# Down product of a SwiGLU block: loads of the rows' tiles issued by ScalarE, and four loading steps tied to named products

## The chip, the cores and the metric

The kernel runs on one core of a Trainium2 chip. The metric is the device time of one execution in microseconds (us). Three runs of the kernel before gave 2198.46, 2200.58 and 2203.82 us; the median is 2200.58 us. A further execution, the one that was profiled, took 2203.5 us.

## The reference

A decoder trunk of two layers works on 1024 positions of width 1024 in float32. Layer 0 mixes with a short gated convolution, layer 1 with dilated attention; each is followed by a feed-forward block (FFN). The FFN's inner width is 2816, which is 22 tiles of 128.

```
def swiglu(h, w_gate, w_up, w_down):
    return (jax.nn.silu(h @ w_gate) * (h @ w_up)) @ w_down

for i in range(DEPTH):                       # DEPTH = 2
    h = rms_norm(x, mix_norm[i])
    ...                                      # x = x + mixer(h)
    h = rms_norm(x, ffn_norm[i])
    x = x + swiglu(h, ffn_w_gate[i], ffn_w_up[i], ffn_w_down[i])
return rms_norm(x, final_norm)
```

## The kernel before

**Numbers and products.** Each float32 operand is split into a high part (ScalarE, an ACTIVATE copy) and a low part (VectorE, a subtraction), and a product is three matmuls of the split parts (lines L515 to L517; L607, L609 and L610 for the smaller "deep" products). On top of that the kernel multiplies by Strassen's scheme in Winograd's form: a block product is made of seven smaller products, numbered 1 to 7 and made in the order `WINOGRAD = 1, 2, 6, 5, 7, 3, 4`.

**Gate and up.** The class `Strassen` with its subclass `Swiglu` makes gate and up in 22 units, u = 0 to 21. Each unit has products (u, m); for part of them the scheme is applied once more, and such a deep product is written m = 11 to 17 (`DEEPER` = 10 plus its number). The list `order` sets the order of all products. The last eleven are those of unit 21: (21,6), (21,5), (21,7), (21,11), (21,12), (21,15), (21,16), (21,3), (21,17), (21,13), (21,14). After (21,7) ScalarE copies the bank to memory (`save`, L521), VectorE adds the other half (L593), multiplies with the gate (L1135), and GpSimd's queue stores the 256 KB half page to DRAM (L674, "plain<-c"). Deep products are taken out of their banks by VectorE (L525).

**Down.** `down` (L728 to L755) multiplies the result by w_down, with the rows in chunks of three pairs. For each m of `WINOGRAD` it makes two products on TensorE, each taken out of its bank by an addition to x on VectorE (L736, "the x-add"). The first two products with m = 6 go to the banks that those with m = 1 used, so they wait for the x-adds of m = 1. Its weights pass through the same engines: L138 makes the high and L139 the low part of a weight tile, L186 forms the combinations.

**The rows' tiles.** The inputs of `down` come back from DRAM. The generator `feed` (L705 to L724) does this in eight steps. The step for an m takes three half pages named "hin" (128x512 float32, 256 KB) and issues their loads (L712), and then it converts the tiles of the step before: three copies on ScalarE (L507) and three subtractions on VectorE (L508). A trio below means these three instructions on one of the engines. There are 63 loads in each FFN, 126 in all.

**What sets the order.** Each engine executes its instructions in the order in which the kernel writes them, and semaphores make it wait for others. The next step of `feed` is called in two ways: `down` calls it after each pair of products, and for the first chunk `filled` calls it after certain products of unit 21 (L780). Before the change these are the five from (21,16) on: (21,16), (21,3), (21,17), (21,13), (21,14). The loads of weights (`load_raw`, L152, "raw") and of x (`load_x`, L702) are on SyncE's queue (SP), as the "hin" loads are. All half pages are taken in turn from one ring of buffers, so a load may have to wait for the last user of its buffer, which can be a store.

Of the kernel before, what the change touches and what calls it, by code (L numbers as in the profile page):

```python
# [28 lines left out]
MAXDIST = 2048  # L29
WINOGRAD = (1, 2, 6, 5, 7, 3, 4)  # L30
DEEP, DEEPER = (2, 4), 10
WARM = 10


# [61 lines left out]
def trunk(ctx: ExitStack, tc: tile.TileContext, x, gains_in, cwi, ck, cwo, wqkv, wo, relb,  # L96
          wg, wu, wd, oneh, ident, out):
    nc = tc.nc
# [11 lines left out]
    def half_page(name, dt=F32):  # L110
        return scope["pool"].tile([128, 512], dt, name=name, tag="half", bufs=scope["halves"])

    def bank():
        return psum.tile([128, 512], F32, name="bank", tag="bank")
# [44 lines left out]
    def ensure(upto):  # L159
        while op_state[0] < min(upto + 1, len(ops)):  # L160
            key = ops[op_state[0] + 1][0] if op_state[0] + 1 < len(ops) else None
            if key in sums_of:
                sums_of.pop(key)()
            made[op_state[0]] = ops[op_state[0]][1]()
            op_state[0] += 1
# [195 lines left out]
    def run(*gens):  # L361
        for _ in zip(*gens):
            pass
        for g in gens:
            for _ in g:
                pass
# [116 lines left out]
    class Strassen:  # L483
# [220 lines left out]
        def feed(self, c):  # L704

            tiles = None
            for m in WINOGRAD + (None,):
                new = None
                if m:
                    new = [half_page("hin") for k in range(self.chunk)]  # L710
                    for k in range(self.chunk):
                        nc.sync.dma_start(new[k], self.parts[c + k, m])  # L712
                if tiles:
                    lows = [self.hi(last, k, t, nc.vector)
                            for k, t in enumerate(tiles)]
                    for lo in lows:
                        lo()
                tiles, last = new, m
                if m:
                    self.b[m] = [None] * self.chunk  # L720
                    yield
# [8 lines left out]
        def down(self, c, n, feed):  # L730

            p, r = {}, {}
            later = {2: (1,), 6: (3,), 5: (4,), 7: (6,), 3: (5,), 4: (7,)}

            def add(n, h, b):
                nc.vector.tensor_tensor(out=X[n][:, half(h)], in0=X[n][:, half(h)], in1=b, op=ALU.add)  # L736

            for m in WINOGRAD:
                for k in (n, n + 2):
                    if m == 1:  # L740
                        p[k] = bank()
                    if m == 5:
                        r[k] = bank()
                    b = bank() if m == 2 else r[k] if m in (3, 5) else p[k]
                    self.mm((c, k), m, b, m in (1, 2, 5), 4)
                    add(k + (m in (5, 7, 4)), int(m in (6, 5, 7, 3)), b)
                next(feed, None)
                if c == n == 0:
                    self.load_x(*later.get(m, ()))
                    self.rest(m)  # L750
# [10 lines left out]
        def run(self, start, hooks={}):  # L761

            self.base = op_state[1]
            last = self.nu - 1

            def filled(n):
                start(n)
                if self.key != CONV:
                    self.now = n + 1
                    i = self.order.index((3, 4))  # L770
                    if n == i - 15:
                        prep.append(self.deepen(2))
                    if n == i - 5:
                        prep.append(self.deepen(4))
                    for p in prep:
                        next(p, None)
                if self.key == CONV:
                    self.below(n, last)
                else:
                    if self.order[n][0] == last and n >= self.at(last, DEEPER + 6) - self.base:  # L780
                        next(feed, None)
                    if self.order[n] == (last, DEEPER + 7):
                        self.load_x(0, 2)
                        ensure(self.at(last, DEEPER + 4) + 4)
                self.idle(n)

            prep = []
            if self.key == CONV:
                self.products(filled, hooks)
                self.first_tiles()  # L790
                return
            feed = self.feed(0)
            self.products(filled, hooks)
            for c in range(0, self.pairs, self.chunk):
                self.down(c, 0, feed)
                feed = self.feed(c + self.chunk) if c + self.chunk < self.pairs else self.feed_last()
                self.down(c, 4, feed)
            run(feed)
# [863 lines left out]
    warm = bank()  # L1662
    for _ in range(WARM):
        nc.tensor.matmul(warm[:, :128], ones, ones, start=True, stop=True)
# [158 lines left out]
```

## Time and profile before

| | |
|---|---|
| median of three runs | 2200.58 us |
| profiled execution | 2203.5 us |
| its span | 2201.7 us |
| granted clock of TensorE, mean | 0.987 |
| TensorE busy | 2143.2 us, 97% |
| VectorE busy | 1762.2 us, 80% |
| ScalarE busy | 997.6 us, 45% |
| "hin" loads | 126 of 256 KB, all on SP |

The profile lists engines as PE (TensorE), DVE (VectorE), ACT (ScalarE), POOL (GpSimd) and SP (SyncE); a "q" behind the name means its DMA queue. Times count from the start of the span. In rows of a timeline the first number is the start and the second the duration, "x3" says that three instructions stand in the row, and the bracket at the end gives the idle time of the engine before it and what ended that. The change lies at two places: from 754 us on, where the first FFN passes from gate and up to down, and from 1946 us on, where the second one does.

### The profile page before, as it was taken

How to read it: one execution, taken by the hardware profiler on the slowest of the kernel's cores; microseconds unless marked ns; L12 is line 12 of the kernel's file. 1: busy time of each engine (PE TensorE's matmuls, PEld its weight loads, DVE VectorE, ACT ScalarE, POOL GpSimd, SP SyncE). 2: the span in 40 equal slices, each digit the busy share in tenths (PEclk: the TensorE clock that was granted, in tenths of full speed). 3: DMA queues.
4: the chain of work that ended last, by engine and by line, in shares of the span. 5: the costliest groups of instructions: out<-in, count | busy, mean ns of one | idle time of the engine just before them, and what ended most of it. 6: DMA issues, size and time to landing. Idle time of an engine off the chain costs nothing.

```text
span 2201.7 us, 30568 instructions
## 1 busy us (share of the span) xinstructions
PE 2143.2 (97%) x11158; PEld 1832.0 (83%) x11158; DVE 1762.2 (80%) x3242; ACT 997.6 (45%) x1800; POOL 153.2 (7%) x202
## 2 busy tenths in 40 slices
PE   9999999899999999999999999998899999999998
PEld 7788877688888878878999998887778888878887
DVE  7898759888888798865677777868988888889886
ACT  7433426444444444435455455534544444454435
POOL 1000000010101000010111111110010101000000
PEclk9999999999999999999999999999899999999999
DMA  7222631223333374323333333443123333265432
GB/s 222 82 91 68 224 121 39 91 96 106 110 97 119 123 280 147 113 67 130 91 91 92 94 98 89 153 148 132 53 79 105 104 105 112 96 233 198 158 91 77
DMA packets 132560, 260.03 MB, mean 118 GB/s; under 512 B 47530, under 2 KB 58810, under 8 KB 132410
## 3 DMA queue, kind: packets, MB, share of 16 engines
q1 hardware_dynamic: 76410, 186.38, 26.6%
q0 software_dynamic: 14832, 48.60, 6.4%
q10 hardware_dynamic: 41168, 23.10, 3.7%
q8 instruction: 88, 1.44, 0.3%
q14 instruction: 62, 0.51, 0.1%
HBM read 188.62 MB, written 66.26 MB: 116 GB/s over the span
## 4 chain that ended last, share of the span: by engine, by line
PE 80%; DVE 11%; ACT 4%; DMA 3%; issue 2%; ACTq 0%; SPq 0%; DVEq 0%
PE bank L517 16%; PE bank L515 16%; PE bank L516 16%; PE bank L356 5%; PE bank L358 5%; PE bank L357 5%; PE bank L1446 4%; PE bank L609 2%; PE bank L610 2%; PE bank L607 2%; DVE w L139 1%; DVE b L508 1%; PE bank L1374 1%; PE bank L1373 1%; DVE x L448 1%
## 5 line engine op out<-in xcount | busy, mean ns | idle before, releaser
L515 PE MATMUL bank<-b,w 128*128 128x512 f32 x1784 | 703.9, 395 | 14.3 <-ACT b L507 6.0
L517 PE MATMUL bank<-b,w 128*128 128x512 f32 x1784 | 702.1, 394 | 15.6 <-DVE w L139 15.6
L516 PE MATMUL bank<-b,w 128*128 128x512 f32 x1784 | 701.5, 393 | 2.6 <-DVE b L508 2.1
L517 PEld LDWEIGHTS bank<-b,w 128*128 128x128 f32 x1784 | 338.9, 190 | 91.0 <-DVE w L139 20.3
L515 PEld LDWEIGHTS bank<-b,w 128*128 128x128 f32 x1784 | 339.2, 190 | 88.5 <-ACT w L138 7.5
L516 PEld LDWEIGHTS bank<-b,w 128*128 128x128 f32 x1784 | 339.0, 190 | 73.8 <-DVE b L508 2.9
L138 ACT ACTIVATE w<-combo 128x512 fp32r<-128x512 f32 (+2 forms) x464 | 235.1, 535 | 289.2 <-DVE combo L186 280.2
L139 DVE TENSOR_TENSOR w<-combo,w 128x512 fp32r<-128x512 f32 (+2 forms) x464 | 261.3, 576 | 74.6 <-ACT w L138 71.9
L521 ACT ACTIVATE part<-bank 128x512 f32<-128x512 f32 x168 | 99.5, 595 | 271.9 <-PE bank L517 268.0
L139 DVE TENSOR_TENSOR w<-raw,w 128x512 fp32r<-128x512 f32 (+2 forms) x316 | 169.2, 561 | 21.1 <-ACT w L138 19.4
L525 DVE TENSOR_TENSOR part<-part,bank 128x256 f32<-128x256 f32 (+1 forms) x348 | 159.3, 488 | 28.9 <-PE bank L517 17.1
L138 ACT ACTIVATE w<-raw 128x512 fp32r<-128x512 f32 (+2 forms) x316 | 150.1, 520 | 45.5 <-PE bank L517 11.4
L736 DVE TENSOR_TENSOR x<-x,bank 128x512 f32<-128x512 f32 x168 | 114.6, 682 | 31.2 <-PE bank L517 31.2
L356 PE MATMUL bank<-w_hi,w 128*128 128x512 f32 (+1 forms) x320 | 121.5, 380 | 0.0
L358 PE MATMUL bank<-w_hi,w 128*128 128x512 f32 (+1 forms) x320 | 119.5, 373 | 0.7 <-DVE w L139 0.7
L357 PE MATMUL bank<-w_lo,w 128*128 128x512 f32 (+1 forms) x320 | 119.6, 374 | 0.0
L448 DVE TENSOR_TENSOR x<-x,bank 128x512 f32<-128x512 f32 (+1 forms) x104 | 66.0, 642 | 62.0 <-PE bank L358 53.0
L356 PE MATMUL bank<-h_hi,w_hi 128*128 128x512 f32 x256 | 104.6, 408 | 0.6 <-ACT w_hi L138 0.6
L186 DVE TENSOR_TENSOR combo<-raw 128x512 f32<-128x512 f32 (+1 forms) x160 | 103.2, 645 | 0.0
L358 PE MATMUL bank<-h_hi,w_lo 128*128 128x512 f32 x256 | 100.1, 391 | 0.8 <-DVE w_lo L139 0.8
L357 PE MATMUL bank<-h_lo,w_hi 128*128 128x512 f32 x256 | 99.9, 390 | 0.0
L1132 ACT ACTIVATE part<-part 128x512 f32<-128x512 f32 x66 | 39.7, 628 | 111.5 <-DVE part L525 111.5
(243 smaller groups left out, 3841.3 us busy)
## 6 DMA issues: line engine op xcount, KB each, us to landing
hin<-part SPq DMA_DIRECT2D x126, 256.0 KB
raw<-in_ffn_w_gate SPq DMA_DIRECT2D x44, 512.0 KB
raw<-in_ffn_w_up SPq DMA_DIRECT2D x44, 512.0 KB
part<-sum POOLq DMA_DIRECT2D x72, 256.0 KB, 3.0
raw<-in_ffn_w_down SPq DMA_DIRECT2D x48, 384.0 KB
raw<-in_conv_w_in SPq DMA_DIRECT2D x24, 512.0 KB
x<-spill SPq DMA_DIRECT2D x24, 512.0 KB
raw<-in_attn_w_qkv SPq DMA_DIRECT2D x24, 512.0 KB
```

The lines of the kernel that those rows point to most:

```text
L138: nc.scalar.activation(hi, src, AF.Copy)
L139: eng.tensor_tensor(out=lo, in0=src, in1=hi, op=ALU.subtract)
L186: eng.tensor_tensor(out=c, in0=a, in1=b, op=op)
L356: nc.tensor.matmul(b, whi[:, a], ahi[:, s], start=first, stop=False)
L357: nc.tensor.matmul(b, whi[:, a], alo[:, s], start=False, stop=False)
L358: nc.tensor.matmul(b, wlo[:, a], ahi[:, s], start=False, stop=last)
L515: nc.tensor.matmul(b, hi[:, a], bhi, start=start and k == 0, stop=False, skip_group_check=True)
L516: nc.tensor.matmul(b, hi[:, a], blo, start=False, stop=False, skip_group_check=True)
L517: nc.tensor.matmul(b, lo[:, a], bhi, start=False, stop=k == n - 1, skip_group_check=True)
L521: nc.scalar.activation(t, b, AF.Copy)
L525: nc.vector.tensor_tensor(out=t, in0=t, in1=b, op=ALU.add)
L736: nc.vector.tensor_tensor(out=X[n][:, half(h)], in0=X[n][:, half(h)], in1=b, op=ALU.add)
```

## The change

```
+FEEDING = 5, 7, 3, DEEPER + 4
...
         def feed(self, c):
...
                     for k in range(self.chunk):
-                        nc.sync.dma_start(new[k], self.parts[c + k, m])
+                        nc.scalar.dma_start(new[k], self.parts[c + k, m])
...
                 else:
-                    if self.order[n][0] == last and n >= self.at(last, DEEPER + 6) - self.base:
+                    if self.order[n] in [(last, m) for m in FEEDING]:
                         next(feed, None)
```

All 126 "hin" loads move from SP's queue to ScalarE's, where they stand in order among its ACTIVATEs. In each FFN four steps instead of five are made in unit 21: after (21,5), (21,7), (21,3) and (21,14). The first loads m = 1. The second loads m = 2 and converts m = 1, the third loads m = 6 and converts m = 2, the fourth loads m = 5 and converts m = 6. Before, the trios of m = 1, 2, 6 and 5 were called after (21,3), (21,17), (21,13) and (21,14). The trios of m = 5, 7, 3 and 4 now fall into `down`, behind the products of m = 1, 2, 6 and 5; before, those of 7, 3 and 4 did, behind 1, 2 and 6. The order on TensorE and GpSimd is unchanged. Lines of the kernel after are one higher.

The first place is ScalarE behind the product (21,7), in the first FFN. `part<-bank` saves this product, `w<-combo` are high parts of weights, `b<-hin` is a trio, and `part_0_2` to `part_2_2` are the tiles for m = 2 of pairs 0, 1 and 2. Semaphores called DMASW count GpSimd's transfers, DMAHW those of SP and ScalarE. Before:

```order
L521 ACTIVATE part<-bank 128x512 [waits DMASW1_49,PE_49]
L138 ACTIVATE w<-combo 128x256 x2
L138 ACTIVATE w<-combo 128x512 [waits DVE_49,Activation_49]
L138 ACTIVATE w<-combo 128x256 x4
L507 ACTIVATE b<-hin 128x512 [waits DMAHW5_49,Activation_49]
L507 ACTIVATE b<-hin 128x512 [waits DMAHW6_49]
L507 ACTIVATE b<-hin 128x512 [waits DMAHW7_49]
```

After:

```order
L522 ACTIVATE part<-bank 128x512 [waits DMASW6_49,PE_49,Activation_49]
L713 DMA hin<-part_0_2_182 128x512 [waits DVE_49]
L713 DMA hin<-part_1_2_189 128x512 [waits DMASW0_49,DVE_49]
L713 DMA hin<-part_2_2_196 128x512 [waits DMASW3_49]
L508 ACTIVATE b<-hin 128x512 [waits DMAHW3_49]
L508 ACTIVATE b<-hin 128x512 [waits DMAHW4_49]
L508 ACTIVATE b<-hin 128x512 [waits DMAHW5_49]
L139 ACTIVATE w<-combo 128x256 x2
L139 ACTIVATE w<-combo 128x512 [waits DVE_49]
L139 ACTIVATE w<-combo 128x256 x4
```

Three loads and the trio of m = 1 now stand ahead of the weights of the deep product (21,16), the row `w<-combo 128x256 x2`. The count of DMASW3 that the third load waits for is that of GpSimd's store of the product (21,7), "plain<-c": the load's buffer is the one that this store reads.

The second place is VectorE at the same product. `c` is the result of (21,7), the row `combo<-raw,combo` and the one behind it make the weights of (21,16), and the first `part<-part,bank` empties the bank of (21,11), which (21,16) then uses. Before:

```order
L593 TENSOR_TENSOR c_6767<-part,bank 128x512
L1135 TENSOR_TENSOR c_6654<-c_6767,c_6654 128x512
L186 TENSOR_TENSOR combo<-raw,combo 128x512
L139 TENSOR_TENSOR w<-combo,w 128x256 x2
L525 TENSOR_TENSOR part<-part,bank 128x256 x2
```

After:

```order
L594 TENSOR_TENSOR c_6773<-part,bank 128x512
L1136 TENSOR_TENSOR c_6654<-c_6773,c_6654 128x512
L509 TENSOR_TENSOR b<-hin,b 128x512 x3
L187 TENSOR_TENSOR combo<-raw,combo 128x512
L140 TENSOR_TENSOR w<-combo,w 128x256 x2
L526 TENSOR_TENSOR part<-part,bank 128x256 x2
```

The trio of m = 1 has come in ahead of the weights and the emptying of the bank.

The third place is VectorE from the emptying of the banks of (21,13) and (21,14) to the first x-adds of `down`. Before:

```order
L525 TENSOR_TENSOR part<-part,bank 128x256 x2
L508 TENSOR_TENSOR b<-hin,b 128x512 x3
L525 TENSOR_TENSOR part<-part,bank 128x256 x2
L1135 TENSOR_TENSOR part<-part 128x512 x2
L508 TENSOR_TENSOR b<-hin,b 128x512 x3
L186 TENSOR_TENSOR combo<-raw 128x384
L186 TENSOR_TENSOR combo<-combo,raw 128x384
L139 TENSOR_TENSOR w<-combo,w 128x384
L736 TENSOR_TENSOR x<-x,bank 128x512
```

After:

```order
L526 TENSOR_TENSOR part<-part,bank 128x256 x4
L1136 TENSOR_TENSOR part<-part 128x512 x2
L509 TENSOR_TENSOR b<-hin,b 128x512 x3
L187 TENSOR_TENSOR combo<-raw 128x384
L187 TENSOR_TENSOR combo<-combo,raw 128x384
L140 TENSOR_TENSOR w<-combo,w 128x384
L737 TENSOR_TENSOR x<-x,bank 128x512
```

One trio is left here where two stood; the one of m = 5 has gone behind the first x-adds. Further up, between (21,3) and (21,13), the trios of m = 1 and m = 2 stood before, and only that of m = 2 stands there now.

More of the change, by code (lines that the diff above doesn't have):

```diff
@@ L31 @@
 DEEP, DEEPER = (2, 4), 10
+FEEDING = 5, 7, 3, DEEPER + 4
 WARM = 10
@@ L711, in feed @@
                     for k in range(self.chunk):
-                        nc.sync.dma_start(new[k], self.parts[c + k, m])
+                        nc.scalar.dma_start(new[k], self.parts[c + k, m])
                 if tiles:
@@ L779, in filled @@
                 else:
-                    if self.order[n][0] == last and n >= self.at(last, DEEPER + 6) - self.base:
+                    if self.order[n] in [(last, m) for m in FEEDING]:
                         next(feed, None)
```

## The prediction

> **What bounds the kernel now.** I read the page first, then TensorE's waits around the two places of the change, then the timelines of TensorE and VectorE there. The page's first lines:
>
> ```profile
> span 2201.7 us, 30568 instructions
> PE 2143.2 (97%) x11158; PEld 1832.0 (83%) x11158; DVE 1762.2 (80%) x3242; ACT 997.6 (45%) x1800; POOL 153.2 (7%) x202
> ```
>
> TensorE works 97% of the span, so only its idle time, and the time in which it runs at half clock, can be won or added. What it waited for in the first FFN's transition and the start of its down product (740 to 960 us), then in the second's (1900 to 2140 us); columns are total, count, longest:
>
> ```profile
> PE bank L515 <- ACT b L507: 3.0, 1, 3.0
> PE bank L607 <- DVE part L525: 2.0, 1, 2.0
> ```
>
> ```profile
> PE bank L515 <- ACT b L507: 3.0, 1, 3.0
> PE bank L607 <- ACT b L507: 2.0, 1, 2.0
> ```
>
> Each transition has two gaps, and both FFNs show the same. No row names a load: TensorE never waits here for weights or rows' tiles to arrive, so bringing loads forward has no wait of its own to remove. TensorE's timeline places the gaps:
>
> ```profile
> 774.60 0.36 PE L607 MATMUL bank<-t,w 128*128 128x256 f32 x1 [2.01 <-DVE part L525]
> ...
> 787.47 0.52 PE L515 MATMUL bank<-b,w 128*128 128x512 f32 x1 [3.02 <-ACT b L507]
> 787.79 0.63 PE L516 MATMUL bank<-b,w 128*128 128x512 f32 x1
> ...
> 791.19 0.39 PE L515 MATMUL bank<-b,w 128*128 128x512 f32 x1
> 791.42 0.40 PE L516 MATMUL bank<-b,w 128*128 128x512 f32 x1
> ```
>
> The second gap has a tail. From 787.47 to 791.19 stand nine matmuls in 3.72 us; at the step of 0.23 (791.19 to 791.42) they would take 2.07. So 1.65 us more are lost. The clock over that stretch, and after a longer gap elsewhere; the columns behind the window are its length, busy times of PE, PEld, DVE, ACT and POOL, PE's granted clock, DMA share and GB/s:
>
> ```profile
> 787.80:791.20 3.40, 3.40 (x10) 2.63 (x9) 3.40 (x7) 3.02 (x7) 0.00 (x0) 0.50 1.03 415
> ...
> 1511.50:1518.00 6.50, 4.54 (x15) 3.96 (x16) 3.79 (x6) 2.58 (x5) 0.00 (x0) 0.50 0.21 81
> ```
>
> VectorE's timeline says what the gaps wait for:
>
> ```profile
> 761.89 0.69 DVE L593 TENSOR_TENSOR c<-part,bank 128x512 f32<-128x512 f32 x1 [2.27 <-ACT part L521]
> 762.61 0.69 DVE L1135 TENSOR_TENSOR c<-c,c 128x512 f32<-128x512 f32 x1
> 763.22 0.68 DVE L186 TENSOR_TENSOR combo<-raw,combo 128x512 f32<-128x512 f32 x1
> ...
> 764.49 0.75 DVE L525 TENSOR_TENSOR part<-part,bank 128x256 f32<-128x256 f32 x2
> ...
> 769.76 0.69 DVE L525 TENSOR_TENSOR part<-part,bank 128x512 f32<-128x512 f32 x1 [0.59 <-PE bank L517]
> ...
> 771.09 1.89 DVE L508 TENSOR_TENSOR b<-hin,b 128x512 fp32r<-128x512 f32 x3
> ...
> 774.04 0.75 DVE L525 TENSOR_TENSOR part<-part,bank 128x256 f32<-128x256 f32 x2
> ...
> 783.31 1.89 DVE L508 TENSOR_TENSOR b<-hin,b 128x512 fp32r<-128x512 f32 x3
> ...
> 786.64 0.68 DVE L736 TENSOR_TENSOR x<-x,bank 128x512 f32<-128x512 f32 x1
> ```
>
> From 769.76 to the x-add VectorE is not idle. The first gap ends when the bank of (21,17) is emptied (774.04), behind the trio of m = 1 (771.09). The second ends at 787.47, right behind the x-add of 786.64 to 787.32, which frees the bank that the first product of m = 6 takes; the profile names ScalarE's L507, but no trio made then belongs to that product. This x-add stands behind the trios of m = 1, 2, 6 and 5.
>
> **The change part by part: what it wins.** Between the end of (21,3) and the first x-add VectorE loses two trios, those of m = 1 and m = 5, 2 x 1.89 = 3.78 us. The second gap, 3.02, is smaller, so it closes, and with it goes its tail. The gain is 3.0 + 1.65 = 4.7 us in each FFN. The first gap stays: the trio of m = 2 stands where that of m = 1 stood. What is late next there is TensorE itself: VectorE then has 3.78 - 3.02 = 0.8 us to spare.
>
> **What it adds: a wait on ScalarE.** The second step is called right behind (21,7). On ScalarE its three loads and the trio of m = 1 stand ahead of the weights of (21,16), and the third load waits for GpSimd's store of (21,7). Before, the same wait stood on SP, where nothing but loads is queued behind it. The store on POOL, its landing time in the first and in the second FFN, that of an earlier store with little traffic, and SP's wait for it before:
>
> ```profile
> 763.60 0.54 POOL L674 DMA_DIRECT2D plain<-c  x1 [19.99 <-DVE c L1135]
> ```
>
> ```profile
> plain<-c POOLq DMA_DIRECT2D x1, 256.0 KB, 3.9
> ```
>
> ```profile
> plain<-c POOLq DMA_DIRECT2D x1, 256.0 KB, 3.6
> ```
>
> ```profile
> plain<-c POOLq DMA_DIRECT2D x1, 256.0 KB, 2.5
> ```
>
> ```profile
> SPq L712 <- DMA plain<-c: 0.9, 1, 0.9
> ```
>
> The store lands at L = 763.60 + 2.5 to 3.9 = 766.1 to 767.5. I take 3.4, nearer to the rows of this very store, hence L = 767.0; it is a bit under 3.6 because part of the loads now runs ahead of it. Does a DMA issue on ScalarE's queue hold back the ACTIVATE behind it? Rows of ScalarE elsewhere, and the line of its other stores (minimum, median, maximum in ns):
>
> ```profile
> 1003.99 7.32 ACTq L1591 DMA_DIRECT2D spill<-x  x5
> 1011.36 2.96 ACT L138 ACTIVATE w_hi<-raw 128x1024 fp32r<-128x1024 f32 x3 [6.96 <-DMA spill<-x]
> ```
>
> ```profile
> L1203 ACTq DMA_DIRECT2D spill<-x x32: 326/326/343, 305.5 to 1539.0; - x32
> ```
>
> It does: ScalarE was idle for 6.96 us while five issues went out, and its next ACTIVATE started 0.05 us behind the last. So from about 763.7 to L ScalarE stands. VectorE stands as well, since the trio of m = 1 is its next row and needs ScalarE's copies, and then TensorE, whose (21,16) needs weights and a bank from both. ScalarE's rows:
>
> ```profile
> 761.75 0.71 ACT L138 ACTIVATE w<-combo 128x256 fp32r<-128x256 f32 x2
> ...
> 765.77 1.66 ACT L507 ACTIVATE b<-hin 128x512 fp32r<-128x512 f32 x3
> ```
>
> and (21,16) on TensorE:
>
> ```profile
> 765.37 0.28 PE L607 MATMUL bank<-t,w 128*128 128x256 f32 x1
> ```
>
> The chain behind L: issue of the load 0.33, ScalarE's trio 1.66, the third subtraction on VectorE 1.89 / 3 = 0.63, together 2.6. Then as before: from L186 at 763.22 to the bank's emptying at 764.49 1.27 us, and from there to (21,16) at 765.37 0.88 us. (21,16) starts at L + 4.75 = 771.75 instead of 765.37: a new gap of 6.4 us, with L's bounds 5.5 to 6.9. ScalarE's weights for it (0.71) fit beside VectorE's work. The gap passes on in full, since at 769.76 VectorE waited for TensorE.
>
> **The clock behind the new gap.** It is longer than both gaps above. Behind that of 3.02 the clock was 0.50 for 3.4 us, costing 1.65; behind the row at 1511.50 it was 0.50 for 6.5 us, costing 3.2 in a dense stretch. I take 1.7, with 0 and 3.2 as bounds: VectorE empties the banks of (21,3) and (21,17) here and may be late anyway. In the Trainium skill, the page "TensorE: Matmul & The Clock Gate" (section "Part 1: The HAM clock gate") says that an idle window of about 3.4 us brings the half clock and a busy one of the same length ends it. By that rule the cost is 1.7; by the longer row it is 3.2, and 3.0 more in the sum over two FFNs. The row at 787.47 differs from the page in another point: 3.02 us of idling sufficed.
>
> **The later steps.** In `down` the trio of m = 5 comes on top of VectorE's work, 1.89 us. Windows of the first FFN, same columns:
>
> ```profile
> 790.00:820.00 30.00, 30.00 (x131) 24.75 (x130) 27.05 (x51) 11.16 (x23) 0.00 (x0) 0.98 0.59 195
> 820.00:850.00 30.00, 30.00 (x134) 24.84 (x133) 29.93 (x55) 15.74 (x32) 0.00 (x0) 1.00 0.52 173
> ```
>
> Up to 820 VectorE has 2.95 us left and TensorE misses nothing, so most of it is hidden; if that cover is gone it costs all 1.89. I take 0.5 of 0 to 1.9. ScalarE gets three issues of 0.33, 1.0 us, in each step of `down`. In 820 to 850 it was idle for 14.26 us; a step has two products of nine matmuls, 4.1 us, so that is 1.9 us a step. I take nothing; the other end is the last rival.
>
> **The sum.** For each FFN 6.4 + 1.65 + 0.5 - 4.7 = +3.9 us; bounds 5.5 + 0 + 0 - 4.7 = +0.8 and 6.9 + 3.2 + 1.9 - 4.7 = +7.3. Two FFNs: +7.8, from +1.6 to +14.6. The profiled execution took 2203.5 us, its span 2201.7; it would become 2211.3. It lies 2.9 above the median of the runs, so the median becomes 2200.58 + 7.8 = 2208.4, from 2202.2 to 2215.2. About 0.3%, or 6.6 us, is the least that a measurement of this kernel can tell from no change.
>
> **The rivals.** *The wait does not hold ScalarE (not slower).* If ACTIVATEs pass the waiting issue, or the store lands before ScalarE gets there, no gap opens at (21,16), and only the gain is left: 2 x (0.5 - 4.7) = -8.4, 2192.2 us. For it speaks that L1203's issues cost 0.33 us each; against it the idle 6.96 us above. It decides from a gap of about 2.5 us (with its half clock) downward, for then the gain is larger. In the Trainium skill, "DMA: Bandwidth & Descriptors" (section "Issuing engines are not separate DMA queues") says that issuing from several engines saves only the time of issuing, as all share the same DMA engines. Read as the whole price of moving the loads, the sum by it is that of this rival; the 6.96 us show that the page leaves out what stands behind the issue.
>
> *Gain and loss cancel.* The gap is at its short end (5.5) and the clock does not drop, or VectorE's own lateness swallows the drop: +0.8 in each FFN, 2202.2 us. For it speaks the store of 2.5 us; against it both rows of this store.
>
> *ScalarE is late all through `down`.* In the first rows above ScalarE's five issues took 7.32 us, 1.46 each, not 0.33. If the loads' issues are slowed like that, or wait for buffers, the copies come late for VectorE, which is full from 820 on. At 0.4 us in each of 34 steps (42 groups of three loads, less the eight in unit 21) this adds 14 us: 2222 us. Against it speak three issues of 256 KB in a step, not eight, and ScalarE's idle half. It decides from the point at which a step's issues exceed the 1.9 us that ScalarE has left in it.
>
> **How the numbers follow.** Forecast 0.60, of which I put 0.37 above +6.6 us and 0.23 below it; no hold 0.15; cancelled 0.17; ScalarE late 0.08. Slower by over 0.3%: 0.37 + 0.08 = 0.45. Within 0.3%: 0.23 + 0.17 = 0.40. Faster: 0.15. The range takes in the bounds of the sum and reaches half into the first rival, and some way toward the last: 2192 to 2218.
>
> **What would show it.** In the profile of the changed kernel: ScalarE and VectorE idle from about 764 to 767 us with the store's landing as releaser; a gap of 5.5 to 6.9 us at (21,16) and half clock behind it; the gap of 2.0 still ahead of (21,14); none of 3.0 ahead of the first m = 6; the same in the second FFN. The prediction is wrong if (21,16) starts without a gap, if the 3.0 us remain, or if new gaps run through `down`.

## The result, and the profile after

The kernel after took 2213.41 us (median of 6 runs, 2209.69 to 2214.59), the kernel before 2200.32 us in the same comparison. The ratio is 1.0056, 95% interval 1.0043 to 1.0069: the change makes the kernel slower by about 13 us, where 7.8 were forecast. The profiled execution took 2211.88 us.

What TensorE waits for in the kernel after, first in the first FFN (740 to 960 us), then in the second (1900 to 2140 us); the columns are total, count, longest:

```profile
PE bank L608 <- DVE part L526: 8.0, 2, 6.0
PE bank L516 <- DVE x L737: 0.9, 1, 0.9
```

```profile
PE bank L608 <- DVE part L526: 8.1, 2, 6.1
PE bank L516 <- DVE x L737: 0.9, 1, 0.9
```

The wait of 3.0 ahead of the first product with m = 6 is gone. The gap of 2.0 ahead of (21,14) is still there, and a gap of 6.0 stands beside it. TensorE's timeline shows where:

```profile
766.78 0.55 PE L608 MATMUL bank<-t,w 128*128 128x256 f32 x1 [6.01 <-DVE part L526]
...
778.31 0.36 PE L608 MATMUL bank<-t,w 128*128 128x256 f32 x1 [2.01 <-DVE part L526]
```

The first is (21,16), the second (21,14). ScalarE's timeline shows the cause of the first:

```profile
756.55 0.60 ACT L522 ACTIVATE part<-bank 128x512 f32<-128x512 f32 x1 [2.29 <-issue]
756.57 5.86 ACTq L713 DMA_DIRECT2D hin<-part  x3
762.48 1.67 ACT L508 ACTIVATE b<-hin 128x512 fp32r<-128x512 f32 x3 [5.33 <-DMA plain<-c]
```

Three issues stretch over 5.86 us, and ScalarE does nothing for 5.33 us until GpSimd's store lands, as the bracket says. VectorE stands with it, for its next rows need these copies; then come the weights and the bank for (21,16):

```profile
763.14 1.90 DVE L509 TENSOR_TENSOR b<-hin,b 128x512 fp32r<-128x512 f32 x3 [4.54 <-ACT b L508]
764.95 0.69 DVE L187 TENSOR_TENSOR combo<-raw,combo 128x512 f32<-128x512 f32 x1
765.55 0.76 DVE L140 TENSOR_TENSOR w<-combo,w 128x256 fp32r<-128x256 f32 x2
766.22 0.75 DVE L526 TENSOR_TENSOR part<-part,bank 128x256 f32<-128x256 f32 x2
```

The granted clock (the number ahead of the DMA share and GB/s at the end) behind the gap of 6.0 and behind that of 2.0:

```profile
766.80:770.20 3.40, 3.40 (x14) 3.30 (x15) 3.40 (x11) 3.40 (x10) 0.00 (x0) 0.50 0.98 380
...
778.30:781.70 3.40, 3.39 (x15) 3.21 (x16) 3.37 (x9) 0.37 (x1) 0.00 (x0) 0.54 0.02 5
```

The gap of 2.0 is now followed by a stretch at half clock. In the kernel before the same gap was not:

```profile
774.60:778.17 3.57, 3.57 (x21) 3.20 (x22) 3.54 (x8) 0.00 (x0) 0.00 (x0) 1.00 1.02 405
```

The order on TensorE is unchanged, so each matmul of the kernel before has its counterpart after. The difference of their start times, taken from the end of (21,15) on, shows step by step where the time goes. The kernel before had come to this place 4.76 us later in its profiled execution, a difference that arose in the first 330 us, far ahead of the change; the steps do not contain it.

| matmul | first FFN, start before and after | step | step in the second FFN |
|---|---|---|---|
| (21,16), first | 765.37, 766.78 | +6.17 | +6.28 |
| (21,17), first | 769.56, 773.27 | +2.30 | +2.38 |
| (21,14), first | 774.60, 778.31 | 0.00 | 0.00 |
| down, the 10th | 778.17, 783.43 | +1.54 | +1.56 |
| down, first of m = 6 | 787.47, 789.56 | -3.17 | -3.18 |
| nine further | 791.19, 791.60 | -1.68 | -1.61 |
| later in down | 811.86, 813.47 | +1.21 | +1.30 |
| sum | | +6.4 | +6.7 |

Both FFNs together give +13.1, which is also the difference of the medians.

### The profile page after: what moved, and what is told of

Same layout as the page of the kernel before. It is cut to its first block, busy times and chain, and to the rows that moved or that the text cites. A ratio compares the mean times of both kernels' runs of the same rounds, so it can differ in the third digit from the quotient of the medians.

```text
span 2209.8 us, 30489 instructions
## 1 busy us (share of the span) xinstructions
PE 2146.1 (97%) x11158; PEld 1835.3 (83%) x11158; DVE 1763.3 (80%) x3242; ACT 1001.2 (45%) x1800; POOL 153.6 (7%) x202
## 4 chain that ended last, share of the span: by engine, by line
PE 50%; issue 30%; DVE 10%; ACT 4%; POOL 3%; DMA 2%; ACTq 0%; SPq 0%; POOLq 0%; DVEq 0%
PE bank L518 8%; PE bank L516 8%; PE bank L517 8%; PE bank L359 5%; PE bank L357 5%; PE bank L358 5%; PE bank L1447 4%; POOL part L698 2%; DVE b L509 2%; DVE w L140 1%; PE bank L1375 1%; PE bank L1374 1%; POOL part L679 1%; DVE x L449 1%; PE bank L1315 1%
```

## The experiments

Each kernel was timed against the kernel before in five rounds; the ratio is that of the kernel to before. An edit can shift line numbers by one or two, so the x-add is L736 to L739.

**The steps alone.** The kernel after, with the loads on SP.

```
-                        nc.scalar.dma_start(new[k], self.parts[c + k, m])
+                        nc.sync.dma_start(new[k], self.parts[c + k, m])
```

> The four named steps of the kernel after, but the loads of the rows' tiles on SP's queue as in the kernel before. Theory (the cost comes from ScalarE standing behind one load that waits for a store): with the wait back on SP only the trio of m = 1 (1.9 us on VectorE) stands ahead of (21,16), so the gap there falls from 6.0 to about 1.9 us with little or no half clock behind it, the gap of 3.0 ahead of m = 6 and its tail stay away (-4.5), the later gap in the down product costs 0.5 to 1.1: for each FFN -1.5 to -2, a median of 2196 to 2198 us, slightly faster than before. Rival (the places of the steps cost, whatever the queue): still slower than before by 8 us or more, over 2208.

Measured: 2196.66 us, ratio 0.9986 (0.9976 to 0.9995). TensorE's waits in the first FFN:

```profile
PE bank L608 <- DVE part L526: 3.4, 2, 2.0
```

The two waits are 2.0 ahead of (21,14) and the rest, 1.4, at (21,16). The steps at their new places win 3 to 4 us; the queue turns that into a loss.

**The queue alone.** The kernel before, with the loads on ScalarE.

```
-                        nc.sync.dma_start(new[k], self.parts[c + k, m])
+                        nc.scalar.dma_start(new[k], self.parts[c + k, m])
```

> The steps of the kernel before, with all 126 loads on ScalarE's queue. Theory: the load that needs the buffer of GpSimd's store comes two products later, when the store has landed, so ScalarE is not held: both gaps of before (2.0 and 3.0 us) stay and nothing of 6 us appears at (21,16); the median stays within 3 us of before, 2198 to 2204. Rival (the issues on ScalarE make its copies late all through the down product): new gaps in down, over 2208 us.

Measured: 2200.46 us, ratio 1.0000 (0.9992 to 1.0009). The 126 issues on ScalarE cost nothing where none of them waits long. So neither half of the change costs anything by itself.

**One load back on SP.** The kernel after, but the load that waits for the store on SP.

```
-                        nc.scalar.dma_start(new[k], self.parts[c + k, m])
+                        (nc.sync if (c, k, m) == (0, 2, 2) else nc.scalar).dma_start(new[k], self.parts[c + k, m])
```

> The kernel after, with one load of 63 in each FFN put back on SP's queue: the third of m = 2 for pairs 0 to 2, which waits for the store. Theory: this one load holds ScalarE, so the gap at (21,16) falls from 6.0 to about 2 us and most of the half clock behind it goes; with -4.5 for the gap and tail ahead of m = 6 and +1.1 in down this is -1.5 to +0.5 for each FFN, a median of 2197 to 2202 us. Rival (the other 62 loads and the trio, not this wait): little changes, over 2208 us.

Measured: 2206.10 us, ratio 1.0023 (1.0014 to 1.0032), between the two expectations. The gap at (21,16) fell to 3.6 and 3.3 us, not to 2. ScalarE's and VectorE's timelines say why:

```profile
758.87 1.68 ACT L508 ACTIVATE b<-hin 128x512 fp32r<-128x512 f32 x3 [1.85 <-DVE c L1136]
```

```profile
759.54 1.89 DVE L509 TENSOR_TENSOR b<-hin,b 128x512 fp32r<-128x512 f32 x3 [1.07 <-ACT b L508]
762.45 0.69 DVE L187 TENSOR_TENSOR combo<-raw,combo 128x512 f32<-128x512 f32 x1 [1.01 <-DMA plain<-c]
```

The second load, still on ScalarE, waits for VectorE's product with the gate. And the store's buffer was given to another tile: VectorE itself now waits for the store, 1.01 us. The edit did not take the wait away but moved it; it could not settle the question. The profiled execution took 2202.28 us, the shortest of the eleven, so these gaps and the clock behind them need not stand for the median.

**The third step later.** The kernel after, with its third step behind (21,17).

```
-FEEDING = 5, 7, 3, DEEPER + 4
+FEEDING = 5, 7, DEEPER + 7, DEEPER + 4
```

> The kernel after, with its third step called after (21,17) instead of (21,3). VectorE then empties the bank of (21,17) ahead of the trio of m = 2, so the gap of 2.0 us ahead of (21,14) should close. Theory on the clock (the second stretch at half clock is set off by that gap): 2.0 + 1.5 us go in each FFN, a median of about 2206.5 us. Rival (the half clock there is a late effect of the gap of 6 us): the 2.0 us go but 1.5 stay, about 2209.5 us.

Measured: 2212.86 us, ratio 1.0055 (1.0043 to 1.0068): nothing won on the kernel after, so both forecasts of the time failed. TensorE's waits in the first FFN:

```profile
PE bank L608 <- DVE part L526: 7.1, 2, 6.9
PE bank L516 <- DVE x L737: 4.0, 4, 1.6
```

The gap ahead of (21,14) did close (7.1 less 6.9 is 0.2), but waits for x-adds grew from 0.9 to 4.0 us in down, and the gap at (21,16) was longer by 0.9. On the clock the trace sides with the theory all the same: behind (21,14), where the kernel after showed 0.54, the granted clock was full, and so it was in the second FFN.

```profile
777.20:780.60 3.40, 3.40 (x21) 3.06 (x22) 3.37 (x8) 0.00 (x0) 0.00 (x0) 1.00 0.12 46
```

So a gap of 2.0 and a stretch at half clock went, and the time stayed. That led to a second theory: from (21,3) to about 20 us into down VectorE has hardly any idle time (in the kernel after, from 773.47 to 803.4 us, no row shows more than 0.23), so its work sets when this stretch ends, and a gap of TensorE closed inside it comes back. Three kernels with the loads on SP tested it.

**The third step later, on SP.** The steps alone, with the same edit of `FEEDING`.

```
-FEEDING = 5, 7, 3, DEEPER + 4
+FEEDING = 5, 7, DEEPER + 7, DEEPER + 4
```

> The named steps with the loads on SP's queue, the third step after (21,17) instead of (21,3). Theory (in the first 20 us of down VectorE has no idle time, so a gap closed ahead of it comes back as a wait for x-adds): the gap of 2.0 ahead of (21,14) closes, waits for x-adds of together about 2 us appear in down, and the median stays within 2 us of the named steps on SP: 2195 to 2198 us. Rival (TensorE's gaps add up): 2 x 2.0 us are won, about 2192.5 us.

Measured: 2196.44 us, ratio 0.9984 (0.9976 to 0.9993), the same as the steps alone. TensorE's waits in the first FFN:

```profile
PE bank L516 <- ACT b L508: 2.1, 3, 1.2
PE bank L608 <- DVE part L526: 1.6, 2, 1.4
```

That is 1.8 us less at (21,14), 3.4 before and 1.6 now, and 2.1 us more in down. The profile names ScalarE's copies as what ended the waits in down, but each of the three ends 0.15 us behind the end of the x-add that frees the bank; the first of them on VectorE and on TensorE:

```profile
781.53 0.68 DVE L737 TENSOR_TENSOR x<-x,bank 128x512 f32<-128x512 f32 x1
```

```profile
782.36 0.47 PE L516 MATMUL bank<-b,w 128*128 128x512 f32 x1 [1.22 <-ACT b L508]
```

**The first step earlier, on SP.** The steps after (20,3), (21,5), (21,17) and (21,14).

```
-FEEDING = 5, 7, 3, DEEPER + 4
+FEEDING = (-1, 3), (0, 5), (0, DEEPER + 7), (0, DEEPER + 4)
...
-                    if self.order[n] in [(last, m) for m in FEEDING]:
+                    if self.order[n] in [(last + d, m) for d, m in FEEDING]:
```

> The loads on SP's queue and the steps after (20,3), (21,5), (21,17) and (21,14): the trio of m = 1 falls ahead of the end of (21,7), where VectorE was idle for 2.3 us. Theory (VectorE's work sets the end of this stretch): no gap at (21,16), gaps ahead of (21,14) and m = 6 closed, and beside the named steps on SP another 1.9 us of VectorE's work in each FFN lie where it was idle: 2196.7 - 2 x 1.9 = about 2193 us. Rival (TensorE's gaps add up): 2.0 + 4.7 - 0.5 for each FFN, about 2187.5 us.

Measured: 2192.83 us, ratio 0.9970 (0.9958 to 0.9982). It is faster than the kernel before by 7 us and than the kernel after by about 20. VectorE's timeline:

```profile
753.48 1.90 DVE L509 TENSOR_TENSOR b<-hin,b 128x512 fp32r<-128x512 f32 x3
...
757.03 0.69 DVE L594 TENSOR_TENSOR c<-part,bank 128x512 f32<-128x512 f32 x1 [0.30 <-ACT part L522]
```

The trio of m = 1 fills the idle time ahead of the end of (21,7): 0.30 us are left of 2.27.

**The first step earlier, the third at (21,3).** The same, with `(0, 3)` in place of `(0, DEEPER + 7)`.

```
-FEEDING = (-1, 3), (0, 5), (0, DEEPER + 7), (0, DEEPER + 4)
+FEEDING = (-1, 3), (0, 5), (0, 3), (0, DEEPER + 4)
```

> As the kernel with the early first step, but the third step after (21,3). Theory (VectorE's work sets the end): the gap of 2.0 us ahead of (21,14) is back, yet the median stays within 1.5 us of that kernel, about 2193 us. Rival (TensorE's gaps add up): 4 us above it.

Measured: 2193.54 us, ratio 0.9972 (0.9962 to 0.9982). TensorE's waits in the first FFN:

```profile
PE bank L608 <- DVE part L526: 2.0, 1, 2.0
PE bank L516 <- ACT b L508: 0.5, 1, 0.5
```

The gap of 2.0 is back, the wait in down is 0.5 instead of 2.1, and the time is the same. All three agree with the second theory.

**Conversions ahead of the loads, in every step.** All loads stay on ScalarE.

```
-                    for k in range(self.chunk):
-                        nc.scalar.dma_start(new[k], self.parts[c + k, m])
                 if tiles:
...
                     for lo in lows:
                         lo()
+                if m:
+                    for k in range(self.chunk):
+                        nc.scalar.dma_start(new[k], self.parts[c + k, m])
```

> The kernel after with one thing turned round in every step of feed: the conversions of the step before come first, the three loads behind them. All 126 loads stay on ScalarE's queue and the steps at the same products. The load that follows (21,7) third then gets another buffer and waits for a subtraction on VectorE, not for the store; the store's buffer goes to a load two products later. Theory (the price is what stands on ScalarE behind the wait for the store): the gap at (21,16) falls from 6.0 to 1.5 to 2.0 us, as with the loads on SP, the half clock behind it goes, and with up to 1.1 for late copies in down the median is 2197 to 2200 us, not slower than before. Rival (ScalarE's 63 issues in each FFN cost by themselves): over 2204 us.

Measured: 2212.76 us (2201.35 to 2215.84), ratio 1.0051 (1.0033 to 1.0069). The gap at (21,16) fell to 1.4 us in both FFNs, as the theory had it, but the median is the rival's. The reason is new. In all later steps the loads are now issued behind the copies, and the next step's copies wait for them: in 2000 to 2140 us ScalarE waited

```profile
ACT b L508 <- DMA hin<-part: 19.0, 19, 2.2
```

against 9.4 us in 9 waits in the kernel after, and TensorE waits for x-adds, in the second FFN for 7.1 us:

```profile
PE bank L516 <- DVE x L738: 7.1, 3, 2.7
```

**Conversions first, in one step.** So the order was turned round only in the step behind (21,7).

```
-                    for k in range(self.chunk):
+                    for k in range(self.chunk if (c, m) != (0, 2) else 0):
                         nc.scalar.dma_start(new[k], self.parts[c + k, m])
...
                         lo()
+                for k in range(self.chunk if (c, m) == (0, 2) else 0):
+                    nc.scalar.dma_start(new[k], self.parts[c + k, m])
```

> The kernel after, with conversions ahead of loads in one step only, the one behind (21,7) (and nowhere in down, where turning them round made the loads late). All loads on ScalarE, steps at the same products; the load behind (21,7) no longer takes the buffer of the store. Theory (ScalarE held by that one wait is the price of the change): gap at (21,16) 1.5 us, little half clock, the rest of down as in the kernel after: -2 + 1.2 for each FFN, a median of 2196 to 2200 us. Rival (the named steps and the queue together cost elsewhere): over 2206 us.

Measured: 2199.56 us, ratio 0.9997 (0.9988 to 1.0006). ScalarE's timeline:

```profile
758.26 0.60 ACT L522 ACTIVATE part<-bank 128x512 f32<-128x512 f32 x1 [2.29 <-issue]
758.75 0.33 ACTq L720 DMA_DIRECT2D hin<-part  x1
758.75 1.66 ACT L508 ACTIVATE b<-hin 128x512 fp32r<-128x512 f32 x3
760.33 0.93 ACTq L720 DMA_DIRECT2D hin<-part  x2
```

No issue waits for the store any more, and TensorE's waits ahead of (21,16) and (21,14), the first row, are those of the steps alone; the second row is a wait in down:

```profile
PE bank L608 <- DVE part L526: 3.4, 2, 2.0
PE bank L516 <- DVE x L739: 1.1, 1, 1.1
```

Three loads and three copies trading places once in each FFN take back the whole loss on the kernel before, from 2213.41 to 2199.56 us, with every load still on ScalarE. That settles the cause of the loss. The kernel is still 2.9 us above the steps alone on SP. In the profiled executions this shows in the first FFN as the wait of 1.1 for an x-add, which the steps alone do not have there, and in the second as a stretch at half clock behind the gap of 2.0 (granted clock 0.68 over 3.4 us, against 1.00). Why the x-add comes later is not shown.

## Why the prediction was right or wrong

- **Direction and mechanism: right.** The wait was on the load that was named, and ScalarE, VectorE and TensorE stood behind it in the order that was given. That this is the cause, and not one that was only argued, is shown by the last kernel above, with the steps alone and the queue alone beside it.
- **The new gap: right.** 6.0 and 6.1 us, forecast 6.4 in 5.5 to 6.9. The store landed 3.2 and 3.3 us after its issue, where 3.4 was taken.
- **The gap and tail ahead of m = 6: right.** They went, for 3.17 + 1.68 and 3.18 + 1.61 us, where 4.7 was forecast. The gap of 2.0 stayed, also as forecast.
- **The clock behind the new gap: wrong in size.** This is the term that failed: 1.65 us in each FFN, with 0 and 3.2 as bounds. Measured were 2.30 + 1.54 = 3.8 and 2.38 + 1.56 = 3.9, beyond the bound. The forecast took one stretch of 3.4 us behind the gap, as at 787.47. In the trace the half clock began inside the gap and held for 6.83 us, of which 4.94 lay behind the gap. And the gap of 2.0 ahead of (21,14), which cost nothing extra in the kernel before, brought a second stretch. The prediction carried that gap over as unchanged and at no cost; the last section shows that the place of such a gap decides, and not its length alone. The sum stayed within its bounds of 0.8 to 7.3 (6.4 and 6.7 measured) although this term did not, because no other term came to its dear end; that much is luck.
- **The later steps: in the bounds.** 1.2 and 1.3 us, where 0.5 of 0 to 1.9 was taken. The forecast had VectorE's extra trio as the reason. In the kernel after part of it comes from ScalarE's queue: at 803 to 805 us ScalarE waits 0.48 and 0.62 us for loads to land, VectorE 0.42 and 0.56 us for ScalarE's copies, and then TensorE 0.9 us for the x-add. With the steps alone on SP the first FFN shows no wait there, though it has the same stretch at half clock ahead of it.
- **What the forecast was short of.** The clock's 2.2 us too little and the 0.7 in down, in both FFNs, are 5.8 us; the gap forecast too long by 0.2 and the gain measured a little higher take a part back. That is the distance between 7.8 and 13.1. The steps are not independent, though. With the steps alone on SP, by the same differences against the kernel before, the first FFN lost 1.58 us to half clock behind the gap of 2.0 and the second nothing, yet the first won 1.7 us in all and the second 2.1, since in the second 1.1 us came back later in down. So the 1.54 us of the second stretch are where the time shows in the kernel after, and what it would have taken without that stretch is not shown.
- **The rivals.** "The wait does not hold ScalarE" fell with the bracket of 5.33 us. "Gain and loss cancel" did not happen. "ScalarE is late all through down" is out as the cause: the queue alone costs nothing. It came true in the kernel with conversions first in every step, by late loads and not by slow issues.

## What to carry to other kernels

Before a transfer is moved to the queue of an engine that computes, read what each issue waits for in the built order: the wait holds everything that the engine does behind it, and a wait that was free on a queue of loads alone can stop three engines (here ScalarE for 5.33 us, VectorE for 4.54 and TensorE for 6.0). In a stretch where a second engine is full, look for that engine's idle time instead of the first one's gaps: a gap closed inside such a stretch came back here a few microseconds later, and what was won here was work moved out of it. An edit that takes a wait away can hand its buffer to someone else, so look in the trace whether the wait is gone or has moved.

## What the runs showed of the hardware

The half clock does not follow from the length of a gap alone. In each of the eleven traces the clock changes only at points a multiple of 3.41 us apart; the stretch between two such points is called a window here. Where the windows fall against the work differs from trace to trace and from one FFN to the other. Here is the first transition of the kernel after, cut at these points; the two numbers to read are PE's busy time, which stands behind the 3.41, and the granted clock:

```profile
761.49:764.90 3.41, 0.00 (x0) 0.00 (x0) 1.76 (x3) 2.28 (x5) 0.00 (x0) 1.00 0.96 349
764.90:768.31 3.41, 1.53 (x7) 1.56 (x8) 3.41 (x10) 2.64 (x7) 0.00 (x0) 0.50 0.52 186
768.31:771.72 3.41, 3.41 (x13) 2.93 (x13) 2.59 (x8) 3.04 (x8) 0.00 (x0) 0.50 0.83 315
771.72:775.14 3.42, 3.42 (x24) 3.13 (x23) 1.63 (x3) 0.00 (x0) 0.00 (x0) 1.00 0.37 103
775.14:778.55 3.41, 1.40 (x12) 1.23 (x11) 3.41 (x9) 0.00 (x0) 0.54 (x1) 1.00 0.23 89
778.55:781.96 3.41, 3.41 (x15) 3.22 (x15) 3.38 (x9) 0.63 (x2) 0.00 (x0) 0.50 0.02 5
```

The gap of 6.0 fills a whole window, half clock follows, and here it lasts until a window has been busy throughout. The gap of 2.0 lies whole in one window, and half clock follows again. The steps alone show the same gap with both outcomes, in the first FFN and in the second:

```profile
769.53:772.94 3.41, 1.51 (x13) 1.54 (x14) 3.41 (x9) 0.00 (x0) 0.00 (x0) 1.00 1.01 362
772.94:776.35 3.41, 3.41 (x11) 2.64 (x10) 3.38 (x9) 1.91 (x4) 0.05 (x1) 0.50 1.05 407
...
1957.37:1960.78 3.41, 3.12 (x26) 2.88 (x24) 3.08 (x5) 1.35 (x3) 0.54 (x1) 1.00 1.02 396
1960.78:1964.19 3.41, 1.69 (x13) 1.72 (x14) 3.38 (x10) 0.00 (x0) 0.00 (x0) 1.00 0.99 325
1964.19:1967.60 3.41, 3.41 (x16) 2.80 (x16) 3.41 (x9) 2.08 (x4) 0.23 (x1) 1.00 1.06 411
```

In the first FFN 1.90 us of idle time fall into one window, and half clock follows. In the second the windows split the gap into 0.29 and 1.72, and the clock stays full. Over all eleven traces, in the transitions and the down products (740 to 960 and 1900 to 2140 us), half clock followed all 20 windows at full clock in which TensorE was idle for 1.86 us or more, and none of the 1439 others, whose longest idle time was 1.85. This describes these stretches only: elsewhere in the same traces half clock also followed windows with less idle time.

The gap of 2.0 us ahead of (21,14) stands in eight of the profiled kernels, twice in each, and half clock followed it in 8 of 16 cases. All 8 are in kernels with an earlier gap at (21,16), but the split accounts for them without it: in the six cases that have no earlier gap, at most 1.57 us fell into one window. A gap of 3.29 us that was split into 1.7 and 1.6 (one load on SP, second FFN) was not followed by half clock either.

In the Trainium skill, the page "TensorE: Matmul & The Clock Gate" (section "Part 1: The HAM clock gate") says that the window of activity on which the clock is set runs freely, and that the point at which the clock changes depends on where in it the first matmul falls. These rows agree with that.
